# Four 16 KB input slots in place of three, seven output slots with the last pair in the first one's, and casts by row halves in the order a0 b0 a1 b1

**Chip, cores, metric.** One core of one Trainium2 (trn2) chip; the other cores are not used by the program. Times are device microseconds (us) of one execution. Runs are called fast when they lie within 1.5% of the fastest of the same kernel on the same chip.

## The reference

```python
# a: (16, 512, 512) float32 as (batch, k, m);  b: (16, 512, 512) float32 as (batch, k, n)
def reference(a, b):
    return np.matmul(a.transpose(0, 2, 1), b).astype(np.float32)
```

Sixteen independent 512 x 512 x 512 products, 33.5 MB read and 16.8 MB written. The kernel works on pairs of batches: one batch on partitions 0 to 63, the other on 64 to 127.

## The kernel before

```python
G = 2; Q = 64; R = 8; V = 2; RV = 4; T = 4; H = 2; pairs = 8; NX = 3
x_ts   = [pool.tile([P, R, M], f32) for j in range(NX)]          # input slots, 16 KB per partition
abf_ts = [pool.tile([P, RV, M], bf) for v in range(V)]           # bf16 row halves a0, a1
bbf_ts = [pool.tile([P, RV, N], bf) for v in range(V)]           # b0, b1
o_ts   = [pool.tile([P, G, T, N], f32) for j in range(pairs)]    # eight output slots, 16 KB each

# SP: all loads, then all stores, on one queue
for n in range(2 * pairs):                                       # a and b of pair 0, a and b of pair 1, ...
    if n >= NX: nc.sync.wait_ge(s_in, n - NX + 1)                # the slot's old content is cast
    nc.sync.dma_start(x_ts[n % NX][:], in_v[n % 2][n // 2]).then_inc(s_x[n % NX], 16)
for i in range(pairs):
    nc.sync.wait_ge(s_out, i + 1)
    nc.sync.dma_start(out_v[i], o_ts[i][:]).then_inc(s_o, 16)

# VectorE (DVE): casts a0 a1 b0 b1
for n in range(2 * pairs):
    i = n // 2
    nc.vector.wait_ge(s_x[n % NX], 16 * (n // NX + 1))           # the load has landed
    for v in range(V):
        if i and v == 0: nc.vector.wait_ge(s_v, G * i)           # PE is through with the last pair's half 0
        if i and v == 1: nc.vector.wait_ge(s_mm, G * H * i)      # PE is through with the last pair
        nc.vector.tensor_copy(out=(bbf_ts if n % 2 else abf_ts)[v][:],
                              in_=x_ts[n % NX][:, v * RV:(v + 1) * RV, :]).then_inc(s_cast, 1)
    nc.vector.memset(dve_done[:, n:n + 1], 0.0).then_inc(s_in, 1)

# TensorE (PE): per pair 64 matmuls, half 0 after three casts, half 1 after the fourth
for v in range(V):
    if v == 0: nc.tensor.wait_ge(s_cast, 3).then_inc(s_cast, -3)
    else:      nc.tensor.wait_ge(s_cast, 1).then_inc(s_cast, -1)
    # ... for t in T, for r in RV, for g in G: matmul(...)

# ScalarE (ACT): per pair four copies PSUM -> o_ts[i], then s_out  (cut)
```

## Time and profile before

| | before |
|---|---|
| runs first given | 129.17, 130.57, 130.68 us |
| with the runs beside the change | 129.17 to 131.99 us, median 130.62 (6 runs) |
| profiled run | 129.26 us, span 127.4 us |
| busiest | DMA queue 95.5% of 16 engines; PE 47%, DVE 30%, ACT 25% |
| transfers | 24 of 2.097 MB, about 4.89 us each at full flow |

The span is the time from the first to the last instruction. The prediction reads the page, the DMA stretches and the timeline. One more view is needed to compare: the waits of VectorE (engine, line, what it waited for: us in total, times, longest).

```profile
DVE abf L81 <- PE ps L104: 38.4, 14, 4.4
DVE abf L81 <- DMA x<-in_a_dram: 9.2, 1, 9.2
DVE bbf L81 <- DMA x<-in_b_dram: 3.5, 3, 2.5
```

Apart from the first load, the casts waited for PE, hardly ever for data.

### The profile page before, as it was taken

How to read it: one execution, taken by the hardware profiler on the slowest of the kernel's cores; microseconds unless marked ns; L12 is line 12 of the kernel's file. 1: busy time of each engine (PE TensorE's matmuls, PEld its weight loads, DVE VectorE, ACT ScalarE, POOL GpSimd, SP SyncE). 2: the span in 40 equal slices, each digit the busy share in tenths (PEclk: the TensorE clock that was granted, in tenths of full speed). 3: DMA queues.
4: the chain of work that ended last, by engine and by line, in shares of the span. 5: the costliest groups of instructions: out<-in, count | busy, mean ns of one | idle time of the engine just before them, and what ended most of it. 6: DMA issues, size and time to landing. Idle time of an engine off the chain costs nothing. (4 is left out here: it accounts for less than half of the span.)

```text
span 127.4 us, 1263 instructions
## 1 busy us (share of the span) xinstructions
PE 59.6 (47%) x512; PEld 35.0 (27%) x512; DVE 38.1 (30%) x48; ACT 31.8 (25%) x41; POOL 0.4 (0%) x5
## 2 busy tenths in 40 slices
PE   0000099559649739928937945962990000000000
PEld 0000045236336414505615623631650000000000
DVE  0016513373372380373365347337000000000000
ACT  0000000960830740290190091083056000000000
POOL 1000000000000000000000000000000000000000
PEclk9999999999999977999999999999999755555555
DMA  5999999999999999989999999999999999999980
GB/s 93 398 425 422 427 437 442 422 411 437 447 427 411 422 417 427 422 365 324 411 432 288 396 417 437 406 401 422 424 427 429 429 427 427 427 429 429 427 345 15
DMA packets 4625, 50.41 MB, mean 396 GB/s; under 512 B 400, under 2 KB 528, under 8 KB 528
## 3 DMA queue, kind: packets, MB, share of 16 engines
q1 hardware_dynamic: 4480, 50.33, 95.5%
q10 hardware_dynamic: 144, 0.07, 0.2%
q14 instruction: 1, 0.01, 0.0%
HBM read 33.55 MB, written 16.84 MB: 395 GB/s over the span
## 5 line engine op out<-in xcount | busy, mean ns | idle before, releaser
L104 PE MATMUL ps<-bbf,abf 64*128 64x512 bf16 x512 | 59.6, 390 | 36.0 <-PEq L99 36.0
L104 PEld LDWEIGHTS ps<-bbf,abf 64*128 64x128 bf16 x512 | 35.0, 112 | 60.1 <-issue 42.5
L125 ACT COPY o<-ps 128x1024 f32<-128x1024 f32 x32 | 30.1, 1027 | 43.3 <-PE ps L104 43.3
L81 DVE CAST abf<-x 128x2048 bf16<-128x2048 f32 x16 | 19.5, 1227 | 47.6 <-PE ps L104 38.4
L81 DVE CAST bbf<-x 128x2048 bf16<-128x2048 f32 x16 | 18.9, 1222 | 3.5 <-DMA x<-in_b_dram 3.5
L125 ACT ACT_TABLE_LOAD x1 | 1.3, 1283 | 22.6 <-PE ps L104 22.6
L130 ACT ACTIVATE act_done<-act_done 1x1 uint32<-1x1 uint32 x8 | 1.6, 197 | 0.0
L86 DVE MEMSET dve_done<- 1x1 f32 x16 | 0.9, 59 | 0.0
L117 POOL MEMSET o<- 128x128 f32 x1 | 0.2, 204 | 0.5 <-SPq L62 0.5
L145 POOL MEMSET const-bfloat16-1.0<- 128x1 bf16 x1 | 0.1, 101 | 0.0
L145 POOL MEMSET const-uint8-127<- 128x1 uint8 x1 | 0.1, 101 | 0.0
L145 POOL MEMSET const-float32-0.0<- 128x1 f32 x1 | 0.1, 98 | 0.2 <-issue 0.2
L145 POOL MEMSET const-float32-1.0<- 128x1 f32 x1 | 0.1, 98 | 0.0
## 6 DMA issues: line engine op xcount, KB each, us to landing
x<-in_a_dram SPq DMA_DIRECT2D x8, 2048.0 KB, 11.9
x<-in_b_dram SPq DMA_DIRECT2D x8, 2048.0 KB, 9.9
out_dram<-o SPq DMA_DIRECT2D x8, 2048.0 KB, 28.4
out_dram<-o ACTq DMA_DIRECT2D x1, 64.0 KB, 9.3
```

What stands on the lines that cost most here:

```text
L81: nc.vector.tensor_copy(out=(bbf_ts if n % 2 else abf_ts)[v][:], in_=x_ts[n % NX][:, v * RV:(v + 1) * RV, :],).then_inc(s_cast, 1)
L86: nc.vector.memset(dve_done[:, n:n + 1], 0.0).then_inc(s_in, 1)
L104: mm = nc.tensor.matmul(ps_ts[g][h][:, t % 2, :], a_m[:, t], bbf_ts[v][rows, r, :], start=(v == 0 and r == 0), stop=(v == V - 1 and r == R ...
L117: nc.gpsimd.memset(o_ts[0][:, 0, 0, 0:P], 0.0).then_inc(s_z, 1)
L125: ev = nc.scalar.copy(out=o_ts[i][:, g, 2 * h:2 * h + 2, :], in_=ps_ts[g][h][:])
L130: nc.scalar.memzero(act_done[:, i:i + 1]).then_inc(s_out, 1)
L145: nc = _bacc.Bacc("TRN2", target_bir_lowering=False, num_devices=1)
```

## The change

The intent: a fourth input slot lets SP queue loads further ahead. Its 16 KB per partition are those of the eighth output slot, which goes; the last pair's output is put where the first one's was, after that store has landed. The casts are reordered so that PE can begin with the two first halves, cast while it is still at work on the previous pair.

```diff
-    NX = 3
+    NX = 4
+    NO = pairs - 1
-    o_ts = [... for j in range(pairs)]
+    o_ts = [... for j in range(NO)]
+    s_o0 = tc.alloc_semaphore("s_o0")
-            nc.sync.dma_start(out_v[i], o_ts[i][:]).then_inc(s_o, 16)
+            nc.sync.dma_start(out_v[i], o_ts[i % NO][:]).then_inc(s_o if i else s_o0, 16)
-        for n in range(2 * pairs):
-            i = n // 2
-            nc.vector.wait_ge(s_x[n % NX], 16 * (n // NX + 1))
+        for i in range(pairs):
             for v in range(V):
                 ...                       # the two waits on s_v and s_mm stay
-                nc.vector.tensor_copy(...).then_inc(s_cast, 1)
-            nc.vector.memset(dve_done[:, n:n + 1], 0.0).then_inc(s_in, 1)
+                for n in (2 * i, 2 * i + 1):
+                    if v == 0:
+                        nc.vector.wait_ge(s_x[n % NX], 16 * (n // NX + 1))
+                    nc.vector.tensor_copy(...).then_inc(s_cast, 1)
+                    if v == V - 1:
+                        nc.vector.memset(dve_done[:, n:n + 1], 0.0).then_inc(s_in, 1)
-                if v == 0: wait_ge(s_cast, 3) ... else: wait_ge(s_cast, 1) ...
+                nc.tensor.wait_ge(s_cast, 2).then_inc(s_cast, -2)
+            if i == NO:                   # ACT, last pair
+                nc.scalar.wait_ge(s_o0, 16)
-                        out=o_ts[i][...], in_=ps_ts[g][h][:]
+                        out=o_ts[i % NO][...], in_=ps_ts[g][h][:]
```

More of the change, by code (lines that the diff above doesn't have):

```diff
@@ L45 @@
     bbf_ts = [pool.tile([P, RV, N], bf, name=f"bbf{v}") for v in range(V)]
-    o_ts = [pool.tile([P, G, T, N], f32, name=f"o{j}") for j in range(pairs)]
+    o_ts = [pool.tile([P, G, T, N], f32, name=f"o{j}") for j in range(NO)]
     dve_done = pool.tile([1, 2 * pairs], f32, name="dve_done")
@@ L69 @@
             nc.sync.wait_ge(s_out, i + 1)
-            nc.sync.dma_start(out_v[i], o_ts[i][:]).then_inc(s_o, 16)
-        nc.sync.wait_ge(s_o, 16 * pairs)
-        for n in range(2 * pairs):
-            i = n // 2
-            nc.vector.wait_ge(s_x[n % NX], 16 * (n // NX + 1))
+            nc.sync.dma_start(out_v[i], o_ts[i % NO][:]).then_inc(s_o if i else s_o0, 16)
+        nc.sync.wait_ge(s_o0, 16)
+        nc.sync.wait_ge(s_o, 16 * (pairs - 1))
+        for i in range(pairs):
             for v in range(V):
@@ L80 @@
                     nc.vector.wait_ge(s_mm, G * H * i)
-                nc.vector.tensor_copy(
-                    out=(bbf_ts if n % 2 else abf_ts)[v][:],
-                    in_=x_ts[n % NX][:, v * RV:(v + 1) * RV, :],
-                ).then_inc(s_cast, 1)
-            nc.vector.memset(dve_done[:, n:n + 1], 0.0).then_inc(s_in, 1)
+                for n in (2 * i, 2 * i + 1):
+                    if v == 0:
+                        nc.vector.wait_ge(s_x[n % NX], 16 * (n // NX + 1))
+                    nc.vector.tensor_copy(
+                        out=(bbf_ts if n % 2 else abf_ts)[v][:],
+                        in_=x_ts[n % NX][:, v * RV:(v + 1) * RV, :],
+                    ).then_inc(s_cast, 1)
+                    if v == V - 1:
+                        nc.vector.memset(dve_done[:, n:n + 1], 0.0).then_inc(s_in, 1)
         for h in range(H):
@@ L91 @@
             for v in range(V):
-                if v == 0:
-                    nc.tensor.wait_ge(s_cast, 3).then_inc(s_cast, -3)
-                else:
-                    nc.tensor.wait_ge(s_cast, 1).then_inc(s_cast, -1)
+                nc.tensor.wait_ge(s_cast, 2).then_inc(s_cast, -2)
                 for t in range(T):
@@ L125 @@
                     ev = nc.scalar.copy(
-                        out=o_ts[i][:, g, 2 * h:2 * h + 2, :], in_=ps_ts[g][h][:]
+                        out=o_ts[i % NO][:, g, 2 * h:2 * h + 2, :], in_=ps_ts[g][h][:]
                     )
```

## The prediction

> **What bounds the kernel now.** I read the page first (busy shares, the tenths, the DMA queues), then the DMA share in chosen stretches, then the instructions in order of time around the odd stretch.
>
> ```profile
> span 127.4 us, 1263 instructions
> PE 59.6 (47%) x512; PEld 35.0 (27%) x512; DVE 38.1 (30%) x48; ACT 31.8 (25%) x41; POOL 0.4 (0%) x5
> ...
> PEclk9999999999999977999999999999999755555555
> DMA  5999999999999999989999999999999999999980
> GB/s 93 398 425 422 427 437 442 422 411 437 447 427 411 422 417 427 422 365 324 411 432 288 396 417 437 406 401 422 424 427 429 429 427 427 427 429 429 427 345 15
> ...
> q1 hardware_dynamic: 4480, 50.33, 95.5%
> ```
>
> No compute engine is busy for half of the span; the one queue that carries every load and store fills 95.5% of sixteen DMA engines. It carries 24 transfers of 2.097 MB (16 loads, 8 stores, together 50.33 MB), loads first. So the end is: start, plus 24 transfers at full rate, plus the holes in the DMA stream. The GB/s row shows where the holes are: slices 17, 18 and 21 (365, 324, 288), all in the load part; the store part is flat at 427 to 429. The same in stretches of my choice (start and end in us, its length, five engines' busy time, then PE clock, DMA share, GB/s):
>
> ```profile
> 5.00:45.00 40.00, 22.77 (x192) 13.16 (x192) 16.49 (x20) 11.74 (x15) 0.00 (x0) 1.00 1.01 430
> 45.00:57.00 12.00, 8.45 (x64) 4.24 (x64) 5.56 (x9) 4.64 (x8) 0.00 (x0) 0.86 0.98 411
> 57.00:60.00 3.00, 2.22 (x22) 1.51 (x24) 1.62 (x3) 0.16 (x2) 0.00 (x0) 1.00 0.88 279
> ...
> 67.00:72.00 5.00, 4.31 (x40) 2.88 (x42) 2.08 (x4) 0.00 (x0) 0.00 (x0) 1.00 0.96 315
> ```
>
> Why there? The PE clock dips in slices 14 and 15, just before. The timeline gives the chain (start us, us, engine, line, what, and the idle time before it):
>
> ```profile
> 9.22 2.36 DVE L81 CAST abf<-x 128x2048 bf16<-128x2048 f32 x2 [9.22 <-DMA x<-in_a_dram]
> ...
> 14.11 2.36 DVE L81 CAST bbf<-x 128x2048 bf16<-128x2048 f32 x2 [2.53 <-DMA x<-in_b_dram]
> ...
> 36.79 7.10 PE L104 MATMUL ps<-bbf,abf 64*128 64x512 bf16 x64 [2.75 <-PEq L99]
> ...
> 42.17 3.76 ACT L125 COPY o<-ps 128x1024 f32<-128x1024 f32 x4 [6.04 <-PE ps L104]
> 43.93 1.23 DVE L81 CAST abf<-x 128x2048 bf16<-128x2048 f32 x1 [2.16 <-PE ps L104]
> 45.08 1.22 DVE L81 CAST bbf<-x 128x2048 bf16<-128x2048 f32 x1
> ...
> 46.60 8.45 PE L104 MATMUL ps<-bbf,abf 64*128 64x512 bf16 x64 [2.71 <-PEq L99]
> ...
> 56.39 0.33 SPq L66 DMA_DIRECT2D x<-in_b_dram  x1
> ...
> 57.78 2.57 PE L104 MATMUL ps<-bbf,abf 64*128 64x512 bf16 x22 [2.73 <-PEq L99]
> ...
> 86.92 2.36 DVE L81 CAST bbf<-x 128x2048 bf16<-128x2048 f32 x2 [0.67 <-DMA x<-in_b_dram]
> ```
>
> A pair's PE work takes 7.10 us, but the second a-cast waits for its end, the first b-cast comes after that, and PE needs three casts to start: 2.7 us of PE waiting in every pair. The loop PE, a-cast, b-cast, PE takes 46.60 - 36.79 = 9.81 us. The first two loads landed at 9.22 and 14.11, so a load takes 4.89 us and a pair of loads 9.78. The loop is exactly as long as the transfers and has nothing to catch up with. When PE ran one pair in 8.45 us at a lowered clock, everything behind came 1.35 us later: the next b load was issued at 56.39, 11.18 us after the one before it (45.21), and the DMA engines ran dry at 57 to 60. The delay was never won back.
>
> How much was lost? The last b load (16th) would have landed at 9.22 + 15 x 4.89 = 82.6. The cast that waited for it began at 86.92: 4.3 us lost. Of this, 57 to 60 and 67 to 72 account for (430-279) x 3 + (430-315) x 5 = 1028 GB/s us, over 430 is 2.4 us; 45 to 57 for 0.5; the rest lies in small dips between 72 and 88 (417 GB/s).
>
> **What the Trainium skill says.** "DMA: Bandwidth & Descriptors", section "Where 436 GB/s comes from": the fabric's ceiling is 435.2 GB/s, and a 16 MB transfer was measured at 425. This trace holds 427 to 430 for tens of us, so the full stretches have nothing left to gain. "TensorE: Matmul & The Clock Gate", section "What's actually happening": a gate halves PE's clock after an idle window of about 3.4 us, in a free-running window. The trace agrees in size (clock 0.50 from about 46 to 49.4, right after PE's 2.7 us of waiting), but other pairs with the same wait kept full clock, so I take it as an event that may hit any run, once or more. "VectorE: DVE Perf Modes", tier table: an fp32 copy of 2048 elements from SBUF takes 1227 ns; here 1220 to 1228. Reordering the casts won't change their cost. "SBUF", section "Who interferes with whom": DMA does not contend with compute engines; the dips of this trace need no such contention to explain them.
>
> **The change part by part.**
> 1. Cast order a0 b0 a1 b1, PE waiting for two casts per half. Same 32 casts, same 39 us of DVE, no transfer removed. a0 and b0 of the next pair need only the first half of PE's current pair, so they are done before it ends. PE's next start is then bound by its banks: the copies begin 42.17 - 36.79 = 5.38 us after PE's start, and two of the four (3.76 / 2 = 1.88) free the first banks at 7.26. I estimate a loop of about 7.4 us, in place of 9.81, against 9.78 for the loads. PE then waits for data, with 2.4 us to spare per pair; the 1.35 us event fits in. The casts take 4 x 1.15 = 4.6 of 9.78 us.
> 2. Fourth input slot. A load's slot comes free with the second half's casts, two pairs ahead of its use. With a pair's b landing at time t, casts run from t to t + 4.7 in order a0 (already done), b0, a1, b1: the a slot is free at t + 2.4, the b slot at t + 3.6. The queue then still holds the rest of the next a load and the whole next b load. The first bytes of a load flow some 1.6 us after issue (0.94 to about 2.5 at the start), and landing trails the last byte by about 1.8 (2.5 + 4.9 = 7.4 against 9.22). So the load issued at t + 2.4 flows from t + 4.0 at the earliest and is needed at t + 9.8 - 1.8 = t + 8.0: 4 us of reserve, where the kernel before had none.
> 3. Seven output slots. The last pair's copies wait for the first store: landing at about 82.6 + 4.9 = 87.5. Those copies would start at 82.6 + 1.2 + 0.4 + 5.4 = 89.6. The wait is already over; and it isn't on the path, as the last store's turn comes only after seven others, 82.6 + 34.2 = 116.8.
>
> The sum: up to 4.3 us of holes vanish and nothing is added. Last b lands at 82.6, eight stores x 4.89 = 39.1 make 121.7; from there to the span's end I keep what it was before, 127.4 - (86.92 + 39.1) = 1.4. Span 123.1. A second count, by bytes: 50.4 MB at 429 are 117.5, flow starts at 2.5, and full flow stopped at about 123.6 of 127.4, leaving 3.8 for the tail: 123.8. I take 123.4. The profiled run took 129.26 for a span of 127.4, so 1.9 more: 125.3 us.
>
> **The rivals.** (a) The transfers are the bound anyway and deeper prefetch gives nothing. For it: 95.5% of the DMA engines' span. Against it: 4.3 us of holes with a visible cause; the remaining share is the whole gain. It would leave 129 to 130. (b) The holes are the memory's own and not late issues. For it: 67 to 72 is low although its load was issued at 66.20, and slices 22 to 26 wobble. Against: the flat store part and 430 over 5 to 45. If half of the loss were of this kind, 127.4. (c) The wait for the first store delays the last pair by so much that the queue runs dry before the last store. It would need over 20 us; next to nothing for the time. (d) PE's clock gets lowered more often, since PE now waits in one piece for data; each such window costs about 1.35 us of PE and is absorbed unless several follow each other. It could cost 1 us.
>
> **Range and chances.** The three times before are 129.17, 130.57 and 130.68, and the profiled run, with one lowered window, is one of the good ones. I read the others as runs with more lost in the loop; the new kernel shouldn't have that spread. Against 130.57, 125.3 is 4.0% less, against 129.2 3.0%. Rival (b) in half brings it near the 2% line. Low end 124.5 (both counts on the good side), high end 127.3. Faster by over 2%: 0.89; within: 0.10; slower: 0.01.
>
> **What would show it.** Right: no slice below about 400 GB/s between the first and the last; the queue's share at 97 to 99%; the waits list has DVE waiting for the loads pair after pair, where it had DVE waiting for PE (38.4 us); PE's pairs 9.8 us apart with a lowered clock in a window that doesn't shift later loads; the last b cast starts near 83. Wrong: holes at the same size with loads issued well ahead, the read rate below 428 throughout, or a hole before the last store.

## The result, and the profile after

124.80 us median (124.62 to 125.07, 6 runs, all fast), against 130.62 before; the ratio of the fast runs is 0.9603, 95% interval 0.955 to 0.9656. Ratios here are the mean time of one kernel's fast runs over that of the other's of the same rounds, so not quite the ratio of the medians quoted; two of the six runs before (131.95 and 131.99) are slow by the rule above and left out of it. The profiled run took 124.79 us, span 122.8.

The changed kernel's page:

```profile
PEclk9999999999999999999999995999998555555555
DMA  4999999999999999999999999999999999999992
GB/s 85 386 415 437 432 437 443 427 432 437 427 432 427 427 427 427 427 427 427 427 427 427 427 427 427 427 416 427 424 427 427 427 427 427 427 427 427 429 432 101
...
q1 hardware_dynamic: 4480, 50.33, 96.9%
```

The GB/s row is flat; between the ramp of the first two slices and the last one, in which the flow ends, none is below 415. The waits of its VectorE:

```profile
DVE bbf L85 <- DMA x<-in_b_dram: 22.9, 8, 3.7
DVE abf L85 <- PE ps L106: 16.2, 7, 3.5
```

Now the casts wait for each pair's b load, eight times of eight. Its timeline shows one pair, then the pair at a lowered PE clock, then the last b load's cast:

```profile
33.38 1.23 DVE L85 CAST bbf<-x 128x2048 bf16<-128x2048 f32 x1 [2.41 <-DMA x<-in_b_dram]
34.52 1.22 DVE L85 CAST abf<-x 128x2048 bf16<-128x2048 f32 x1
...
35.79 0.33 SPq L68 DMA_DIRECT2D x<-in_a_dram  x1
...
36.94 0.33 SPq L68 DMA_DIRECT2D x<-in_b_dram  x1
...
43.16 1.23 DVE L85 CAST bbf<-x 128x2048 bf16<-128x2048 f32 x1 [3.34 <-DMA x<-in_b_dram]
...
74.06 8.57 PE L106 MATMUL ps<-bbf,abf 64*128 64x512 bf16 x64 [2.69 <-PEq L101]
...
82.31 1.23 DVE L85 CAST bbf<-x 128x2048 bf16<-128x2048 f32 x1 [1.86 <-DMA x<-in_b_dram]
```

With b landing at 33.38, loads were issued 2.41 and 3.56 us later, and the next b landed 9.78 us later: two transfers, no hole. The last b landed at 82.31 where it had been 86.92: 4.61 us sooner, and the span is 4.6 us shorter. All of the gain is in the load part. Some 0.3 us of it was there at the first landing already (8.90 after, 9.22 before); from the first landing to the last it is 77.70 against 73.41 us, so the holes had cost 4.29 us.

How the DMA stream ends shows one thing more. The last stretches before (columns as in the prediction):

```profile
123.00:124.00 1.00, 0.00 (x0) 0.00 (x0) 0.00 (x0) 0.00 (x0) 0.00 (x0) 0.50 0.64 270
124.00:125.00 1.00, 0.00 (x0) 0.00 (x0) 0.00 (x0) 0.00 (x0) 0.00 (x0) 0.50 0.12 49
125.00:126.00 1.00, 0.00 (x0) 0.00 (x0) 0.00 (x0) 0.00 (x0) 0.00 (x0) 0.50 0.04 16
```

and after:

```profile
120.00:121.00 1.00, 0.00 (x0) 0.00 (x0) 0.00 (x0) 0.00 (x0) 0.00 (x0) 0.50 0.49 205
121.00:122.00 1.00, 0.00 (x0) 0.00 (x0) 0.00 (x0) 0.00 (x0) 0.00 (x0) 0.50 0.00 0
```

All sixteen engines together move 427 GB/s, so one moves about 27. Before, the worth of one or two engines (49, then 16 GB/s) still flowed for some 2 us after the others had ended; after, the flow ends within one microsecond. So before, the engines ended out of step. Holes alone do not do this: of the runs below with holes, the order-only ones end with such a tail too (33, then 16 GB/s in the first of them), but one load late, and slots only with 5/4 of the matmuls, have 0 and 16 GB/s left in the microsecond after the flow breaks off, and nothing after that, as the changed kernel has. What puts the engines out of step stays open.

### The profile page after: what moved, and what is told of

Read it like the earlier page. It is cut to its first block, busy times and chain, and to the rows that moved or that the text cites. A ratio compares the mean times of both kernels' runs of the same rounds, so it can differ in the third digit from the quotient of the medians.

```text
span 122.8 us, 1258 instructions
## 1 busy us (share of the span) xinstructions
PE 60.2 (49%) x512; PEld 35.4 (29%) x512; DVE 37.9 (31%) x48; ACT 31.8 (26%) x41; POOL 0.4 (0%) x5
## 3 DMA queue, kind: packets, MB, share of 16 engines
q1 hardware_dynamic: 4480, 50.33, 96.9%
## 5 line engine op out<-in xcount | busy, mean ns | idle before, releaser
L85 DVE CAST bbf<-x 128x2048 bf16<-128x2048 f32 x16 | 19.6, 1224 | 22.9 <-DMA x<-in_b_dram 22.9
```

## The experiments

Theory: the holes were loads issued too late, as three slots left no reserve against a delay of PE; the fourth slot gives one, and the new cast order gives PE time. Rivals: PE's loop of 9.81 us is the cause, and only the new order cures it; the holes are the memory's own; the shared output slot costs a wait.

| run | median us | runs | ratio of fast runs to before's |
|---|---|---|---|
| changed kernel again | 124.74 | 124.69 to 124.89 | 0.9677 |
| slots only | 124.91 | 124.82 to 125.03 | 0.9689 |
| order only | 143.21 | 137.93 to 144.04, one fast | none |
| order only, other chip | 140.12 | 139.45 to 141.09 | 1.0827 |
| order only, half the matmuls | 141.46 | 134.77 to 144.32, one fast | none |
| before, half the matmuls | 124.92 | 124.69 to 125.03 | 0.9686 |
| before, 5/4 of the matmuls | 142.68 | 141.96 to 143.17 | 1.0994 |
| slots only, 5/4 | 134.74 | 133.96 to 135.06 | 1.0363 |
| changed kernel, 5/4 | 124.97 | 124.77 to 125.22 | 0.9629 |
| one load late | 127.13 | 126.63 to 127.45 | 0.9793 |
| four output slots | 125.94 | 125.58 to 126.26 | 0.9757 |
| six input, five output slots | 125.37 | 125.23 to 125.63 | 0.9707 |

The record classes the ratio of each of these runs as unclear, so what follows rests on differences of several us and on the traces, not on the last half per cent. The kernel before ran beside each of them, at 128.3 to 134.9 us. Its scatter is why the ratio of the same kernel is 0.9603 in one set and 0.9677 in another: there the fast runs of before were only 128.34, 128.91 and 129.59.

### The changed kernel again (after_again)

> The changed kernel again, unchanged, as the yardstick on the same chip and in the same rounds: 124.8 us (124.5 to 125.2).

124.74 us. It repeats. Its trace has what the first one lacks, a lowered clock while loads are still to be issued, twice:

```profile
34.78 8.79 PE L106 MATMUL ps<-bbf,abf 64*128 64x512 bf16 x64 [2.27 <-PEq L101]
...
54.36 8.79 PE L106 MATMUL ps<-bbf,abf 64*128 64x512 bf16 x64 [2.69 <-PEq L101]
```

The casts of the b loads around them still came 9.78 to 9.80 us apart, from 33.26 to 82.20: the changed kernel takes in such an event, of 1.69 us here, without a hole.

### The slots alone (slots_only)

```diff
 # against the kernel before
-    NX = 3
+    NX = 4
+    NO = pairs - 1
 # and seven output slots as in the change; casts a0 a1 b0 b1 and PE's waits (3, then 1) untouched
```

> Only the fourth input slot and the shared output slot; casts a0 a1 b0 b1 and PE's waits for three and one as before. Theory (the holes are late issues, and a slot more is a reserve against them): PE's loop stays at 9.81 us and its gaps of 2.7 us stay, but a load is issued about 4.8 us earlier than it must be, so one to three clock events of 1.35 us each leave no hole: 125.0 us (124.6 to 125.8), GB/s row flat at 427. Rival 1 (PE's loop is what must be shortened): 128 to 131. That would make the cast order the working part.

124.91 us, 0.15 us above the changed kernel's mean of the same rounds: nearly all of the gain. The trace happens to hold a lowered clock at a useful moment, with three loads still to be issued. Its timeline and its GB/s row:

```profile
55.89 8.59 PE L107 MATMUL ps<-bbf,abf 64*128 64x512 bf16 x64 [2.75 <-PEq L102]
...
65.81 0.33 SPq L68 DMA_DIRECT2D x<-in_a_dram  x1
```

```profile
GB/s 80 390 420 442 432 426 442 426 437 426 426 426 432 426 426 432 426 426 426 426 432 426 426 437 426 426 413 426 426 426 426 429 426 429 426 426 426 429 432 83
```

The same 8.5 us pair that made a hole before makes none here, and PE's gap of 2.7 us per pair is still there. So do the casts' waits for PE:

```profile
DVE abf L84 <- PE ps L107: 38.4, 14, 4.5
```

They are as long as before (38.4 us), so this view, which the prediction named as a mark, does not tell whether there are holes. The rival that wants PE's loop shortened falls: at this amount of matmul work the fourth slot is enough.

### The cast order alone (order_only, order_again, order_half_pe)

```diff
 # against the changed kernel
-    NX = 4
-    NO = pairs - 1
+    NX = 3
+    NO = pairs
```

> Only the new cast order and PE's waits for two casts; three input slots and eight output slots as before. Theory (both parts are needed to keep the queue filled; a b load's slot now comes free only with the second half's a cast): with a pair's b landing at t, the next pair's b load is issued at t + 2.4, flows from about t + 4.0, while the a load ahead of it has its last byte at about t + 3.1: a hole of about 1 us in every pair, 7 of them, 124.8 + 6.8 = 131.6 us (range 129.5 to 132.5), no gain over before, and the DMA row dips once per pair from the start instead of after a clock event. Rival 1 (PE's loop of 9.81 us alone made the holes): the loop is shortened here, so about 125. Rival 2 (the holes are the memory's own): 129 to 132 like before, with holes where no load was late.

143.21 us, well outside the expected range: worse than before by far. Five of the six runs are slow by the 1.5% rule; the one fast run, 137.93, is still 9 us above the fast runs of before beside it (128.34 to 129.59). The direction of the theory holds (no gain, one hole per pair from the start), its size doesn't. The timeline and the DMA stretches around one hole, from a slow run of 141.58 us:

```profile
37.66 1.23 DVE L85 CAST bbf<-x 128x2048 bf16<-128x2048 f32 x1 [5.90 <-DMA x<-in_b_dram]
...
40.07 0.33 SPq L68 DMA_DIRECT2D x<-in_b_dram  x1
...
50.13 1.23 DVE L85 CAST bbf<-x 128x2048 bf16<-128x2048 f32 x1 [3.35 <-DMA x<-in_b_dram]
```

```profile
39.00:40.00 1.00, 0.82 (x5) 0.36 (x7) 1.00 (x3) 0.00 (x0) 0.00 (x0) 0.50 0.32 131
40.00:41.00 1.00, 1.00 (x8) 0.50 (x6) 1.00 (x3) 0.00 (x0) 0.00 (x0) 0.50 0.08 33
41.00:42.00 1.00, 1.00 (x8) 0.38 (x5) 0.17 (x2) 0.00 (x0) 0.00 (x0) 0.50 1.43 279
42.00:43.00 1.00, 1.00 (x7) 0.37 (x5) 0.00 (x0) 0.00 (x0) 0.00 (x0) 0.50 0.64 246
```

The issue comes 2.41 us after b's landing, as worked out. But it took 10.06 us from issue to landing where I had reckoned 1.6 + 4.9 + 1.8 = 8.3, and the pair took 12.47 us in place of 10.75. At 40 to 41 only 33 GB/s flow, about one engine's worth; I read this as one engine that still finishes the a load while fifteen have nothing to do, which the trace can't prove. After the issue the stream is back near full rate (410) only from 43 on. The order alone thus makes things worse because it holds a's slot until b has landed (a1 is cast after b0), and with three slots it is that very slot which the next b load needs.

Two runs on another chip looked at whether PE's lowered clock, seen in this trace, is what made the difference.

> The order-only kernel again on this chip, as the yardstick for the run with half the matmuls: 141 us (137 to 145). In the first run the slot's release, the idle queue's restart and a straggling DMA engine made 12.5 us per pair; if the straggler (3 us) was that chip's own, this comes to about 132 instead.

> The order-only kernel with half of the matmuls (wrong result on purpose). In the order-only trace PE ran most pairs at a lowered clock, so PE could be what made it slower than the 131.6 that I had worked out. Theory (PE is not in that loop; b's landing, the second a cast, the next b load's issue and its landing are): within 3 us of the order-only run beside it. Rival (PE's lowered clock is in the loop): 125 to 131.

Order only came to 140.12 us there, all four runs fast, so it is not one chip's straggler. In its trace, of a fast run, a b load again took up to 11.3 us from issue to cast, but as little as 7.8 in one pair. With half of the matmuls the median is 141.46, but those runs scatter from 134.77 to 144.32; its one fast run is 5.4 us below the mean of the other kernel's four. Taking PE's work away thus does not bring the time into the 125 to 131 of the rival; my "within 3 us" does not hold between fast runs, and as no trace of that fast run was kept, what made it faster is not shown. The waits of VectorE in the two traces, order only first, tell whether PE is in the loop:

```profile
DVE bbf L85 <- DMA x<-in_b_dram: 36.1, 8, 7.2
DVE bbf L85 <- DMA x<-in_b_dram: 46.7, 8, 6.9
```

In both, the first b cast waited for its load in all eight pairs, and the next b load was issued 2.41 or 2.42 us after the start of that cast; so PE came last in none of them, and the slot's late release remains the cause. Why engines fall out of step by more in some executions stays open: the packets in the trace do not say which engine they are from.

### Half of the matmuls in the kernel before (half_pe)

```diff
-                    for r in range(RV):
+                    for r in range(RV // 2):       # wrong result on purpose; flags and increments moved along
```

> The kernel before with half of the matmuls (two of four k slices per half; wrong result on purpose), nothing else changed: three slots, old cast order. Theory (before, the loads' slots come free too late because PE's pair ends too late): loop 3.6 + 2.7 = 6.3 us, a slot is free 2.4 us after its landing, flows from + 4.0 and is needed at + 8.0: no holes, 125.0 us (124.6 to 125.8). Rival 2 (holes of the memory's own, or of the cast traffic): 128 to 131 as before.

124.92 us with three slots and the old order. The page's GB/s row:

```profile
GB/s 85 369 419 437 437 442 431 437 426 437 437 431 426 426 426 426 431 426 426 426 426 426 426 426 426 426 418 423 431 429 426 426 429 429 426 431 426 426 431 75
```

Loads, casts and stores are the same as before, PE alone is shorter, and the holes are gone. (A pair took PE 5.1 to 6.6 us, at a granted clock of 0.73 in the mean of the span, and not the 3.6 that I had reckoned; it was short enough.) The holes are therefore not the memory's own. Before, PE's end of a pair held the casts, the casts held the slots, the slots held the loads.

### A quarter more matmuls (pe125_before, pe125_slots, pe125_after)

```diff
-                    for r in range(RV):
+                    for k in range(RV + 1):        # k slice 0 twice, wrong result on purpose
+                        r = max(0, k - 1)
```

> The kernel before with a quarter more matmuls (the first k slice of each half multiplied twice; wrong result on purpose): a pair's PE work is 8.9 instead of 7.1 us. Theory (three slots leave no reserve, the old loop is PE plus 2.7 us): loop 11.6 us against 9.78 for the loads; the last b load lands at about 95 instead of 82, and 137 to 139 us (134.5 to 141).

> The same extra matmuls with the fourth slot and the shared output slot, but the old cast order. Theory: loop still 11.6 us, the reserve of one load (4.8 us) is used up after three pairs, holes from the sixth pair on: about 131 us (129 to 133). A rival that holds the slots for everything: 125.

> The same extra matmuls in the changed kernel. Theory: with casts a0 b0 a1 b1 the PE loop is 8.9 + 0.2 = 9.1 us, below the loads' 9.78, so nothing reaches the end: 124.9 us (124.6 to 126). If the new order adds nothing, it equals the slots-only run with the same matmuls (about 131).

142.68, 134.74 and 124.97 us. Here the cast order is worth 9.8 us on top of the slots: with it a pair still fits between two pairs of loads. The first two lie above my ranges. The timeline of the kernel before with the extra matmuls:

```profile
41.48 10.51 PE L105 MATMUL ps<-bbf,abf 64*128 64x512 bf16 x80 [2.71 <-PEq L99]
...
54.70 10.52 PE L105 MATMUL ps<-bbf,abf 64*128 64x512 bf16 x80 [2.71 <-PEq L99]
```

and of the changed one:

```profile
54.42 8.83 PE L107 MATMUL ps<-bbf,abf 64*128 64x512 bf16 x80 [0.96 <-PEq L101]
...
64.22 8.83 PE L107 MATMUL ps<-bbf,abf 64*128 64x512 bf16 x80 [0.97 <-PEq L101]
```

The same 80 matmuls took 10.5 us behind a gap of 2.71 us, as the clock was lowered during most pairs, and 8.83 behind gaps of 0.96 and 0.97. The old loop is then 13.2 us and not the 11.6 that I had used. The order takes away the gap, and with it, in this trace, the lowered clock. How much of the 9.8 us is due to the one and how much to the other was not separated.

### One load late (one_late8)

```diff
-                nc.sync.wait_ge(s_in, n - NX + 1)
+                nc.sync.wait_ge(s_in, 8 if n == 9 else n - NX + 1)
```

> The changed kernel with one load (the fifth pair's b) issued only when the fourth pair's b slot has come free as well, as three slots would do: about 46.7 us instead of 36.9, while the load ahead has its last byte at about 46.3. It measures what one hole costs. If a late issue costs only its lateness (flow 1.6 us after issue): the hole is 2.0 us and the time 126.8. If an idle queue restarts slowly and one DMA engine then trails the others, as the order-only trace suggests (issue to landing 10.1 us): that load lands at 56.8 instead of 52.9, so 3.9 us and 128.7.

127.13 us, 2.2 above the changed kernel with 5/4 of the matmuls on the same chip (124.97), and 2.3 above the unaltered one elsewhere. The stretches:

```profile
47.00:48.00 1.00, 1.00 (x14) 0.63 (x10) 0.00 (x0) 0.00 (x0) 0.00 (x0) 1.00 1.29 229
48.00:49.00 1.00, 1.00 (x12) 0.68 (x10) 0.80 (x1) 0.00 (x0) 0.00 (x0) 1.00 0.36 98
```

That load was issued at 46.55 and its cast began at 54.51, 8.0 us later; the 10 us of the order-only run are not the rule. (With three slots it would have waited for count 7, a's slot, and not 8; so this load is later than that by one cast.) The cast before it had been at 42.99, so it came 1.7 us later than the usual 9.78 us: a single hole costs about its lateness, 2.0 as worked out. The hole is not made good: the next two b casts follow 9.78 and 9.79 us apart. Another 0.6 us went just before the last b cast (84.42, 10.34 us after the one before it), though its load had been issued at 67.91 already; this is not a late load, and its cause is open.

### Fewer output slots, more input slots (out4, in6_out5)

```diff
-    NX = 4
-    NO = pairs - 1
+    NX = 4          # in6_out5: 6
+    NO = 4          # in6_out5: 5;  one semaphore per store, copies of pair i wait for store i - NO
```

> The changed kernel with four output slots in place of seven (one semaphore for each store; the last four pairs' copies wait for stores one to four). This asks what reserve the shared output slot has. Worked out: the first store lands at about 87, so the fifth pair's copies wait from about 60 until 87, PE's sixth pair until 89; sixth, seventh and eighth pairs then run one after the other at about 7.3 us and the last copies end at about 113, while the last store's turn in the queue comes at about 116.5. All loads can still be issued, as their slots come free with casts that need only the fifth pair's matmuls. Theory: 124.8 us (124.5 to 126), although ACT and PE stand for over 20 us. Rival (an output slot shared is a wait on the path): 130 or more.

125.94 us, 1.2 more than the changed kernel elsewhere (it did not run beside it). ACT and PE stood as expected; the timeline of ACT and PE:

```profile
87.13 3.76 ACT L128 COPY o<-ps 128x1024 f32<-128x1024 f32 x4 [31.75 <-DMA out_dram<-o]
...
111.34 3.76 ACT L128 COPY o<-ps 128x1024 f32<-128x1024 f32 x4 [3.80 <-PE ps L105]
```

ACT waited 31.75 us, and almost nothing came of it at the end. The last copies ended at 115.1 and not at 113, as a pair after the long stand ran in 8.56 us. That is about the last store's turn (116.5 less some 1.6 for the issue), and so a small dip: the 38th slice fell to 375 GB/s. The rival's 130 is refuted; a slot shared as in the change has over 20 us of reserve (there the last copies end at 93, and the last store's issue is needed at about 115).

> The changed kernel with six input slots and five output slots, in the same SBUF. Theory (the queue is never empty with four slots, and the rest is transfers at 428 GB/s): nothing more to gain, 124.8 us (124.5 to 125.2). Rival (some of the 5.4 us beside the 24 transfers are still holes of late loads): below 124.3.

125.37 us: no gain from more slots. Its GB/s row is as flat; of the difference to 124.8, 0.3 us are in the span (123.1 against 122.8) and the rest lies outside of it (2.2 us against 1.9 to 2.0). Both kernels of this set have more semaphores; whether that is what lengthens the part outside was not tried.

No version beat the changed kernel.

## Why the prediction was right

- **The bound and the holes.** Right. The 4.3 us of holes were 4.29 us between the first landing and the last; the first landing, 0.3 us earlier by itself, makes it 4.6. The last b cast began at 82.31 (said: 82.6), the span was 122.8 (123.1 by landings, 123.8 by bytes), the time 124.8 (125.3). The count by landings was the better one; the count by bytes took over a tail of 3.8 us in which one or two engines trailed the others, and that tail is shorter here. What the prediction gave as the rest of the 4.3 us, small dips between 72 and 88, comes to 0.5 us at its own rate of 417, so about 0.9 us were not accounted for. It also had one delay of 1.35 us "never won back"; in fact the loss grew from it. The b load cast at 76.35 was 3.6 us late already (9.22 + 13 x 4.89 = 72.8), the last one 4.3. These two were issued 9.81 and 9.91 us after the ones before them, which hardly adds to the delay, but took 10.15 and 10.81 us from issue to cast, where the one before them took 9.78 (56.39 to 66.17). Why that time grew stays open.
- **Part 2, the fourth slot.** Right, and confirmed alone: slots only reached 124.91. The loads were issued at t + 2.41 and t + 3.56 (said: 2.4 and 3.6).
- **Part 1, the cast order.** The mechanism is right, its share in this gain isn't shown: it is worth 0.15 us here. Its PE loop was estimated at 7.4 us; where PE had data and only banks to wait for, with four output slots, pairs began at 98.19 and 105.79, 7.60 us apart. It is insurance: with 5/4 of the matmuls it is worth 9.8 us. The prediction didn't say that either part alone might do; had it asked, it might have found that the order with three slots does harm.
- **Part 3, the shared output slot.** Right: no wait at the end, and even four slots cost little.
- **Rivals.** (a) is refuted by the result, (b) by half the matmuls, (c) by four output slots. (d) came true in a small way and cost nothing. In the profiled run the clock was lowered for one pair after the first, at 74 us, when the last load had been issued at 66.30, so that this trace does not show an event absorbed while loads wait. The repeat's trace does, with two such pairs, and so does the slots-only trace.
- **Marks.** The queue's share is 96.9%, a shade below the 97 to 99 that I had named; the rest came as said, though a lowered clock that shifts no later load is seen only in the repeat's trace. The scatter is gone too, as said: 0.45 us over six runs, against 2.8 before. That the slower runs before lost more in the loop was not shown, as no trace of one was kept.

## What to carry to other kernels

When one queue carries everything, ask what its holes are and who held the slot whose load came late; a loop that is exactly as long as the transfers has no reserve, and one delay in it is paid in full, or more: here one of 1.35 us was followed by a loss of 4.3. A buffer more on the load side can cure that without any engine getting faster. Reordering work can give a second reserve, but look at which slot it holds longer: the same reorder that is harmless with four slots costs some 10 us with three (9 and 11 between fast runs).

## What the Trainium skill lacked or had wrong

- "DMA: Bandwidth & Descriptors", section "Specifications", gives about 0.6 us to the first byte of a load issued from this queue; no view here shows a first byte by itself. No page says how long a queue that ran dry takes to full rate, which is what a late load costs: issued at 40.07, the stream was at 33 GB/s until 41, 279 and 246 in the next two microseconds, and 410 from 43 on; issue to landing took 8.0 us in one run and 10.1 in another, for a 4.9 us transfer.
- No page says how far the DMA engines of one stream can get out of step: before, the worth of one or two engines (49, then 16 GB/s) ran some 2 us after the others; in the changed kernel the flow ended within 1 us. When it happens is open, as runs with holes ended both ways.
- "DMA: Bandwidth & Descriptors", section "Where 436 GB/s comes from", says that the HBM side (about 358 GB/s) binds for transfers between HBM and SBUF. Loads and stores here held 427 to 430 for tens of us. The page's own remark on single-core numbers fits that; the sentence alone misleads.
- "TensorE: Matmul & The Clock Gate", section "What's actually happening", has the clock lowered after an idle window of about 3.4 us. Here gaps of 2.7 us were enough: after 11 of 14 of them in the two runs with 5/4 of the matmuls and the old order (10.5 instead of 8.83 us), and with the usual amount after one of seven before and two of seven with slots only. No pair behind a gap of 0.95 to 1.00 us ran longer, in the three traces that have such gaps.
